# Token-major gates for the 'b' heads, multiplied on GpSimd and turned by DMA transposes in a split-f16 encoder block

## The chip, the cores and the metric

The kernel runs on one core of a Trainium2 chip, as one launch. The metric is the device time of a launch in microseconds (us), lower is better; it is given as the median of several runs. The core has five engines with queues of their own: PE (TensorE, matrix multiplications out of a stationary operand that PEld loads), DVE (VectorE), ACT (ScalarE), POOL (GpSimd) and SP (SyncE, which issues nearly all DMAs here). Each engine runs its instructions in the order in which they stand in the program and waits at each one for what it needs.

## The reference, cut to what matters

One encoder layer on 1024 tokens of width 1024: a combined projection `x @ w_in`, two groups of eight attention heads of 64 columns each, gates, an output projection, and a normalisation.

```python
h = x @ w_in
q_a, k_a, v_a, z_a, q_b, k_b, v_b, z_b = split(h)
y_a = neighborhood_attention(q_a, k_a, v_a, rel_pos_bias)      # 8 heads, window of 8 x 16 tokens of a 16 x 64 grid
y_b = windowed_gqa_with_sink(rotary(q_b), rotary(k_b), v_b, sink_logits)   # 8 query heads, 2 key heads, |i - j| <= 128
mixed = concatenate([y_a * silu(z_a), y_b * silu(z_b)])
y = mixed @ w_out
x = layer_norm(DEEPNORM_ALPHA * x + y, ln_gain, ln_bias)
```

The change touches `y_b * silu(z_b)` and the way in which that product reaches `mixed @ w_out`.

## The kernel before, in words

**Arithmetic.** Large products are made of f16 parts: a value is split into a high and a low f16 part, and a product takes three passes (high by high, high by low, low by high). `x` and `w_in` are split so; so are the softmax weights, and the gated outputs `zt[e]` for `W_out` (`mh[e]`, `ml[e]`). There are eight gated tiles of 128 columns (two heads) by 1024 tokens, f32: `zt[0..3]` for the 'a' heads, `zt[4..7]` for the 'b' heads.

**Projection.** The 21 groups of 128 columns of `w_in` (without the values, which are projected apart) are computed in the order `ORDER`. `project` (L358, matmul at L379) makes a group channel-major: a 128x128 weight tile is the stationary operand, 512 tokens of `x` move past it, and the result stands with the 128 columns on the partitions. A group is two halves of 512 tokens, each 8 steps of the contraction by three passes, so 48 matmuls of 512 columns. The weights of a group come as two pieces of 512 of the contraction rows (`w_split`, L191): ACT makes the high part (L199), POOL scales and subtracts for the low part (L204, L205). In `project`, the second piece is needed only at the thirteenth matmul of a half. `evac` (L318) reads the result out of PSUM: for a gate, `Silu` on ACT for the first three groups of `ORDER`, and otherwise `Tanh` on ACT (L341) with a product on DVE (L342). A 'b' query group (`qb0` to `qb3`) is rotated by `rope` (L305): a copy on ACT, a shuffle on DVE (L312), then two products and a sum on POOL (L313 to L315), after which ACT casts the high part of each head (L259) and POOL subtracts for the low part (L265).

**Prologue and steps.** The values and the first `NPRO = 6` groups of `ORDER` run before the attention (the last rows of the values end at 59 us). Then 128 units of attention follow, units 0 to 63 for 'b' and 64 to 127 for 'a'; a unit is one head with 128 queries. The 15 other groups are filler: `pump_to` puts their matmuls between those of the units by the marks `FILL_AT`. The loop that sets the order is the step loop at L1180: step `i` emits the scores of unit `i` (`stage_qk`: L816, L817 on PE, then the masked sum and minimum on DVE, L826), the exponential of unit `i` on ACT (L842), and for unit `i - 1` the split of its weights into f16 parts (`stage_tr`: high part on ACT L852, low part on DVE L853) and a DMA transpose of both parts, issued by SP (L856). Every fourth step a quad `q` of four units gets its product with the values (`stage_pv`, L881 on PE) some `LP = 6` steps later, and is normalised on DVE (`stage_on`, L887 and L890) into the tile `on`, f32, tokens on the partitions. When both heads of a pair are there, `stage_ot` (L893) turns the tile `on` by four f32 transposes on PE (L901) into PSUM, and DVE multiplies by the gate and writes `zt[e]` (L904 for 'b', one instruction over 128x512; L910 for 'a', two over 128x256).

The scores of unit `i + 4` use the PSUM bank of unit `i`; they wait for the split of that unit (L852, L853), which reads that bank.

**Side work.** What isn't written into the step by hand stands in four queues (`act`, `dve`, `pool`, `sp`): `enq` adds an operation with those it depends on and a priority, and `pop` takes, at its place in a step, a few operations whose dependencies were emitted in earlier steps. `need` emits an operation at once. The weights of `W_out` are loaded, scaled and split there too. `m_queue(e)` (L1009), called at the steps `M_AT = [105, 112, 118, 120]` for `e = 4..7`, splits the gated 'b' tiles: a cast on ACT (L1013) and a subtraction on POOL (L1014) for each half. The 'a' tiles are split at the end (`final`, L1048, by L938 and L939).

**Output.** `out_mms` (L1021, matmul at L1031) multiplies `W_out`: stationary are 128 tokens of `mh[e]` or `ml[e]`, and 512 columns of `W_out` move (128 or 256 in the last pieces). Most of it runs behind the last unit. The normalisation and the stores end the program.

**Buffers that matter here.** `zslot` gives slots for gate tiles; the gain and the bias of the normalisation took such slots at the end, and the gain's load waited for `m_ops[4]` (L1207). The tag `bs` (`BR = 5` buffers) holds the 'a' heads' bias tables, loaded a few steps ahead by `stage_load`.

Of the kernel before, what the change touches and what calls it, by code (L numbers as in the profile page):

```python
# [15 lines left out]
S = 1024  # L16
# [20 lines left out]
ZTAG = {"z3": "zv", "zb3": "zc", "z2": "zs", "zb1": "zd", "zb2": "ze"}  # L37
KO = (2, 3, 4, 5, 6, 7, 0, 1)
X1_AT = ((0,), (1,), (2,), (3, 4), (5,), (6, 7), (), ())
Z3_END = 119  # L40
# [21 lines left out]
def hybrid_block(ctx, tc, xT, x, wt, wv, wo, bias, sink, gain, lbias, cos, sin, bmask, out):  # L62
# [33 lines left out]
    def zslot(name, tag="z"):  # L96
        return zp.tile([128, S], F32, tag=tag, name=name, bufs=3 if tag == "z" else 1)
# [247 lines left out]
        return [o2]  # L345

    def z_col(e):
        i = 0 if e in (4, 0, 5) else 1 if e == 1 else 2
        return zc[:, i:i + 1]

    groups = []
# [1 line left out]
    def new_group():  # L353
        if len(groups) >= 2:
            need(*groups[-2])
        return bank("pj")

    def project(name):  # L358
        n = ORDER.index(name)
        w_split(2 * n + 2)  # L360
        for half in range(2):
            ps = new_group()
            for k in range(KT):
                if k % 4 == 0:
                    need(w_ops[2 * n + k // 4])
                h, l = parts[2 * n + k // 4]
                if n + 2 < NPRO and half == 0 and k == 4:
                    w_scan(2 * n + 4)
                if n + 2 < NPRO and half == 1 and k == 0:
                    w_scan(2 * n + 5)  # L370
                if half == 0 and k == 4:
                    w_split(2 * n + 3)
                if n + 2 < NPRO and half == 1 and k == 6:
                    w_scale(n + 2)
                for i, (a, b) in enumerate(((h, x16h), (h, x16l), (l, x16h))):
                    mv = b[half, k]
                    if name[0] == "q" and name[1] != "b":
                        mv = mv.rearrange("p (r b c) -> p b r c", b=4, r=8)
                    nc.tensor.matmul(ps, a[:, k % 4, :], mv,  # L379
                                     start=(k == 0 and i == 0), stop=(k == KT - 1 and i == 2))  # L380
# [482 lines left out]
    def stage_pv(q):  # L863
        ps = st[q, "o"] = bank("t")
        for m in range(4):
# [14 lines left out]
            for i, (a, b_) in enumerate(mms):  # L880
                nc.tensor.matmul(ps[:, HD * m:HD * m + HD], a, b_, start=(i == 0), stop=(i == len(mms) - 1))  # L881

    def stage_on(q):
# [6 lines left out]
        nc.vector.tensor_mul(on[g, p, h][:, :, j, :], ps[:, :4 * HD].rearrange("p (m e) -> p m e", e=HD),  # L890
                             ri.unsqueeze(2).to_broadcast([128, 4, HD]))

    def stage_ot(q):  # L893
        g, p, j, h = quad(q)
        if j == 0:
            return
        need(*stk_ops.get(f"zb{p}" if g == "b" else f"z{p}", ()))
        ps = bank("t")
        o = on.pop((g, p, h))
        for i in range(4):  # L900
            nc.tensor.transpose(ps[:, 128 * i:128 * i + 128], o[:, i].rearrange("p h e -> p (h e)"), identf)  # L901
        if g == "b":
            z = zt[4 + p][:, 512 * h:512 * h + 512]
            nc.vector.scalar_tensor_tensor(z, ps, z_col(4 + p), z, op0=ALU.mult, op1=ALU.mult)  # L904
        else:
            for i in range(2):
                b = 2 * h + i
                z = zt[p].rearrange("p (r c) -> p r c", c=GW)[:, :, 16 * b:16 * b + 16]
                src = ps[:, 256 * i:256 * i + 256].rearrange("p (r c) -> p r c", c=16)
                nc.vector.scalar_tensor_tensor(z, src, z_col(p), z, op0=ALU.mult, op1=ALU.mult)  # L910

    for b in range(4):
        at(WIN_AT[b], window, b)
# [15 lines left out]

    def m_alloc(e):  # L930
        if e >= 4:
            t = big_tile(f"m{e}", (128, 2, S), F16)
        else:
            t = tiles["fp"].tile([128, 2, S], F16, tag="m", name=f"m{e}", bufs=4)
        mh[e], ml[e] = t[:, 0, :], t[:, 1, :]

    def m_split(e, sl, hi, lo):
        hi(mh[e][:, sl], zt[e][:, sl])  # L938
        lo(ml[e][:, sl], zt[e][:, sl], mh[e][:, sl])  # L939
# [69 lines left out]
    def m_queue(e):  # L1009
        m_alloc(e)  # L1010
        m_ops[e] = []
        for h in (slice(0, 512), slice(512, S)):
            o = enq("act", lambda h=h: nc.scalar.copy(mh[e][:, h], zt[e][:, h]))  # L1013
            m_ops[e].append(enq("pool", lambda h=h: nc.gpsimd.tensor_sub(  # L1014
                ml[e][:, h], zt[e][:, h], mh[e][:, h]), o))

    LT, LP = LTT, LPP
    LO = LP + 4
# [1 line left out]
    NU = len(units)  # L1020
    def out_mms(t, a, ps, es, c=(0, 512)):  # L1021
        o, w = c
        ts, cs = slice(128 * t, 128 * t + 128), slice(o, o + w)
        ps = ps[:, o:o + w]
        for e in es:
            n = WO_SEQ.index((e, a))
            if n in wo_ops:
                need(wo_ops[n], *m_ops.get(e, ()))
            woh, wol = wo_parts[n]
            for i, (lh, rh) in enumerate(((mh[e], woh), (mh[e], wol), (ml[e], woh))):  # L1030
                nc.tensor.matmul(ps, lh[:, ts], rh[:, cs],  # L1031
                                 start=(e == EO[0] and i == 0), stop=(e == EO[-1] and i == 2))
                yield

# [13 lines left out]
    def final():  # L1048
# [5 lines left out]
        for e in EO[4:]:  # L1054
            m_alloc(e)
        for e in EO[4:]:
            m_split(e, slice(0, 512), nc.scalar.copy, nc.vector.tensor_sub)
            for n in (WO_SEQ.index((e, 0)), WO_SEQ.index((e, 1))):
                wo_split(n)
        for e in EO[4:]:  # L1060
            m_split(e, slice(512, S), nc.scalar.copy, nc.vector.tensor_sub)
# [112 lines left out]
    gain_tile = []  # L1174

    def gain_load():
        gain_tile.append(zslot("gb"))
        nc.sync.dma_start(gain_tile[0], gain.partition_broadcast(128))

    clock["step"] = 0  # L1180
    for i in range(-LD, NU + LO):
# [59 lines left out]
        pop("dve", ND if i < M_AT[1] else 2, same=True)  # L1241
        if i < NU:
            stage_exp(units[i])
        pop("act", NA if i < M_AT[0] and len(queues["act"]) < 5 else 2)
        pop("pool", NP)
        pump_to(i + 1)
    pump(10 ** 6)
# [77 lines left out]
```

## Time and profile before

| What | Value |
|---|---|
| Median of 3 runs | 445.71 us (445.67 to 446.71) |
| The profiled execution's own time | 446.49 us |
| Its span in the profile | 444.7 us |
| Mean granted TensorE clock | 0.995 |
| DMA traffic | 81.39 MB, 133841 packets |

A program on one core has one row of each kind. The page gives times in us from the start of the span, and single durations in ns. In the groups of instructions, the last columns are the group's busy time, the mean duration of one, and idle time of the engine in front of them with what ended it. Matmuls overlap: the next one starts before the one before has ended, so their cost is read from how far apart they start, or from the chain of waits, where a run of them appears as one piece. The profiled execution took 1.8 us more than its span, which lies around it.

### The profile page before, as it was taken

The numbers are of one execution on the slowest core, as the hardware profiler recorded it, in microseconds if no ns is written. First come the engines' busy times: TensorE is split into PE (matmuls) and PEld (weight loads), VectorE is DVE, ScalarE is ACT, GpSimd is POOL, SyncE is SP. The second block draws the span as 40 slices with busy tenths as digits, with TensorE's granted clock in tenths as the row PEclk, the third lists the DMA queues.
The fourth block names the chain that finished last, engine by engine and source line by source line (L and its number), as shares of the span: only waits on it lengthen the run. The fifth ranks groups of instructions, "written<-read, shape, count | busy, mean of one in ns | idle before, by whom it ended". The sixth has DMA issues, their size and how long they took to land.

```text
span 444.7 us, 9505 instructions
## 1 busy us (share of the span) xinstructions
PE 437.5 (98%) x3289; PEld 255.5 (57%) x3289; DVE 344.2 (77%) x849; ACT 308.3 (69%) x700; POOL 221.6 (50%) x235
## 2 busy tenths in 40 slices
PE   9999999999999999999999999999999999999994
PEld 8997754444445565655565655656555654444453
DVE  5978967438986898887988888888878837589944
ACT  5759789766499988887868887888778946302401
POOL 0110074646839558866506767765574405205740
PEclk9999999999999999999999999999999999999997
DMA  8921469984659999587978899998999998103612
GB/s 272 390 91 60 145 235 339 336 292 169 213 127 214 206 190 181 98 162 143 164 127 175 169 182 180 213 170 213 192 204 253 167 172 347 55 0 102 232 69 72
DMA packets 133841, 81.39 MB, mean 183 GB/s; under 512 B 101280, under 2 KB 113440, under 8 KB 133536
## 3 DMA queue, kind: packets, MB, share of 16 engines
q1 hardware_dynamic: 133648, 80.64, 75.4%
q8 instruction: 26, 0.43, 0.4%
q14 instruction: 23, 0.19, 0.2%
q10 hardware_dynamic: 144, 0.13, 0.1%
HBM read 50.34 MB, written 9.96 MB: 136 GB/s over the span
## 4 chain that ended last, share of the span: by engine, by line
PE 91%; DMA 3%; POOL 3%; DVE 1%; issue 1%; ACT 1%; SPq 0%; POOLq 0%; DVEq 0%; ACTq 0%
PE ps_pj L379 44%; PE ps_s L1031 9%; PE ps_s L486 6%; PE ps_t L881 6%; PE ps_pj L1031 5%; PE ps_t L1031 5%; PE ps_s L816 4%; PE ps_s L817 4%; PE ps_pj L486 3%; PE ps_t L486 3%; DMA bias<-in_bias 3%; PE ps_t L901 1%; POOL wl L205 1%; PE ps_t L412 1%; POOL ks L295 1%
## 5 line engine op out<-in xcount | busy, mean ns | idle before, releaser
L379 PE MATMUL ps_pj<-xf,wh 128*128 128x512 f16 x672 | 202.1, 379 | 0.1
L379 PE MATMUL ps_pj<-xf,wl 128*128 128x512 f16 x336 | 127.3, 379 | 0.0
L379 PEld LDWEIGHTS <-wh 128*128 128x128 f16 x672 | 63.7, 98 | 60.4 <-DVE ks L263 0.5
L842 ACT ACTIVATE ps_s<-sn,nm 128x385 f32<-128x385 f32 (+3 forms) x128 | 70.1, 548 | 25.1 <-DVE nm L826 24.6
L853 DVE SCALAR_TENSOR_TENSOR split<-ps_s,split 128x384 f16<-128x384 f32 (+2 forms) x128 | 65.7, 513 | 27.5 <-ACT split L852 25.9
L1031 PEld LDWEIGHTS <-m 128*128 128x128 f16 x432 | 40.0, 98 | 41.1 <-DVE m L939 0.2
L852 ACT ACTIVATE split<-ps_s 128x384 f16<-128x384 f32 (+2 forms) x128 | 57.8, 452 | 2.5 <-DMA tr<-split 0.2
L204 POOL TENSOR_SCALAR wr<-wr,wsc 128x512 f32<-128x512 f32 x26 | 20.6, 791 | 68.1 <-ACT wh L199 61.6
L379 PEld LDWEIGHTS <-wl 128*128 128x128 f16 x336 | 32.9, 98 | 37.4
L826 DVE CUSTOM_DVE_ANT_0 sn<-ps_s,bm,nsk 128x384 f32<-128x384 f32 (+1 forms) x64 | 40.7, 636 | 2.0 <-PE ps_s L817 1.7
L1031 PE MATMUL ps_s<-wo,m 128*128 128x512 f16 (+1 forms) x192 | 40.8, 366 | 0.0
L816 PE MATMUL ps_s<-ks,qs 128*128 128x384 f16 (+4 forms) x128 | 39.2, 306 | 0.3 <-DVE qs L263 0.3
L817 PE MATMUL ps_s<-ks,qs 128*128 128x384 f16 (+4 forms) x128 | 39.2, 306 | 0.0
L826 DVE CUSTOM_DVE_ANT_0 sn<-ps_s,bias,sg 128x264 f32<-128x264 f32 (+1 forms) x64 | 35.0, 547 | 4.5 <-issue 1.5
L881 PEld LDWEIGHTS <-tr 128*128 128x128 f16 (+1 forms) x1104 | 36.6, 98 | 2.2
L205 POOL TENSOR_TENSOR wl<-wr,wh 128x512 f16<-128x512 f32 x26 | 32.7, 1257 | 2.2
L788 POOL TENSOR_SCALAR bias<-bias,rsg 128x552 f32<-128x552 f32 (+1 forms) x24 | 19.1, 797 | 23.8 <-DMA bias<-in_bias 22.6
L295 POOL COPY ks<-ks 64x512 f16<-64x512 f16 x40 | 26.0, 661 | 7.1 <-DVE ks L263 2.8
L1086 ACT ACTIVATE sd<-mv,eps 128x1 f32<-128x1 f32 x8 | 2.4, 295 | 36.5 <-DVE mv L1084 35.2
L1031 PE MATMUL ps_pj<-wo,m 128*128 128x512 f16 (+1 forms) x144 | 26.2, 326 | 0.0
L1130 POOL TENSOR_TENSOR xr<-xr,gb 128x512 f32<-128x512 f32 x7 | 9.8, 1396 | 32.4 <-ACT xr L1127 32.4
L842 ACT ACTIVATION_READ_ACCUMULATOR ps_s<-sn,nm 128x1 f32 x128 | 24.4, 190 | 0.0
(188 smaller groups left out, 813.8 us busy)
## 6 DMA issues: line engine op xcount, KB each, us to landing
ws<-in_wt SPq DMA_DIRECT2D x15, 512.0 KB, 5.9
wr<-in_wt SPq DMA_DIRECT2D x26, 256.0 KB, 3.6
wor<-in_wo SPq DMA_DIRECT2D x22, 256.0 KB, 3.5
bias<-in_bias SPq DMA_DIRECT2D x16, 276.0 KB, 3.3
xr<-in_x SPq DMA_DIRECT2D x8, 512.0 KB, 9.6
out<-xr SPq DMA_DIRECT2D x15, 256.0 KB, 2.1
bias<-in_bias SPq DMA_DIRECT2D x8, 368.0 KB, 3.8
wvraw<-in_wv SPq DMA_DIRECT2D x9, 320.0 KB, 5.8
```

The costliest lines, as they stand in the source:

```text
L205: nc.gpsimd.tensor_sub(l, raw, h)
L295: nc.gpsimd.tensor_copy(t[o, sl], t[a, sl])
L379: nc.tensor.matmul(ps, a[:, k % 4, :], mv, start=(k == 0 and i == 0), stop=(k == KT - 1 and i == 2))
L486: nc.tensor.matmul(ps[:, :320], lh[:, ts], rh[:, cs], start=(k == ko[0] and i == 0), stop=(k == ko[-1] and i == 2))
L816: nc.tensor.matmul(ps[:, :m], q, sl[0], start=True, stop=False)
L817: nc.tensor.matmul(ps[:, :m], q, sl[1], start=False, stop=True)
L826: nc.vector.tensor_tensor_reduce(sn[:, :m], ps[:, :m], bias_t, sg[:, c:c + 1], init, op0=ALU.add, op1=ALU.min, accum_out=nm)
L842: nc.scalar.activation(pt[:, :m], sn[:, :m], AF.Exp, bias=nm, scale=-1.0, accum_out=sm[:, k:k + 1])
L852: nc.scalar.activation(hl[:, :m, 0, :c], src, AF.Copy, scale=PSCALE)
L853: nc.vector.scalar_tensor_tensor(hl[:, :m, 1, :c], src, PSCALE, hl[:, :m, 0, :c], op0=ALU.mult, op1=ALU.subtract)
L881: nc.tensor.matmul(ps[:, HD * m:HD * m + HD], a, b_, start=(i == 0), stop=(i == len(mms) - 1))
L1031: nc.tensor.matmul(ps, lh[:, ts], rh[:, cs], start=(e == EO[0] and i == 0), stop=(e == EO[-1] and i == 2))
```

## The change

1. **Projection of the 'b' gates.** `zb0` to `zb3` are made by a new `project_rows`, token-major: a tile of 128 tokens of `x` is the stationary operand and the 128 weight columns move, so a group is 2 x 96 matmuls of 128 columns, with four blocks of tokens one behind the other. Each block goes through all of the contraction, so both weight pieces are needed at the start.
2. **Order.** The groups of the prologue are now zb0, zb1, zb2, kb, qb0, zb3; `z0` and `z1` take the places of `zb2` and `zb3` in the filler.
3. **Gate of 'b'.** `stage_on` multiplies on DVE by the scale of the gate and by one over the sum in one instruction, and a POOL product (`tensor_mul`, 128x256, 16 of them, priority 0.6) multiplies the gate tile by it, tokens on the partitions. `stage_ot` does nothing for 'b': 32 f32 transposes on PE and the 8 DVE products of L904 are gone.
4. **f16 parts of 'b'.** `m_queue` runs at `M_AT = [26, 42, 57, 80]`. For each half, ACT casts the high part and POOL subtracts the low part, both into a tile `hr`, token-major; then SP issues a DMA transpose of 128x1024 f16 that writes the two parts channel-major into `zt[e]` itself. The `hr` tiles take buffers of the tag `bs` (for `e = 7` the gate slot `zv`). `mh`, `ml` are views with a stride.
5. **Ends.** The steps from which two queued operations may be taken stay as they were (`POP2_AT`). The gain and the bias of the normalisation stand in large tiles of their own, and the gain's load waits for nothing.

```diff
-ORDER = ["zb0", "z0", "zb1", "kb", "qb0", "z1", "qb1", "zb2", "qb2", "k0", "qb3", "zb3", "q0", "k1", "q1",
+ORDER = ["zb0", "zb1", "zb2", "kb", "qb0", "zb3", "qb1", "z0", "qb2", "k0", "qb3", "z1", "q0", "k1", "q1",
...
-M_AT = [105, 112, 118, 120]
+M_AT = [26, 42, 57, 80]
+POP2_AT = (105, 112)
...
+    def project_rows(name):
+        n = ORDER.index(name)
+        w_split(2 * n + 2)
+        for half in range(2):
+            ps = new_group()
+            need(w_ops[2 * n], w_ops[2 * n + 1])
+            for c in range(96):
+                t, k, i = c // 24, c // 3 % 8, c % 3
...
+                ts = slice(128 * t, 128 * t + 128)
+                h, l = parts[2 * n + k // 4]
+                a, b = ((x16h, h), (x16l, h), (x16h, l))[i]
+                nc.tensor.matmul(ps[:, ts], a[half, k][:, ts], b[:, k % 4, :], start=(c % 24 == 0), stop=(c % 24 == 23))
+                if c % 4 == 3 and c < 95:
+                    yield
+            groups.append(evac(name, half, ps))
+            yield
...
-        nc.vector.tensor_mul(on[g, p, h][:, :, j, :], ps[:, :4 * HD].rearrange("p (m e) -> p m e", e=HD),
-                             ri.unsqueeze(2).to_broadcast([128, 4, HD]))
+        o, src = on[g, p, h][:, :, j, :], ps[:, :4 * HD].rearrange("p (m e) -> p m e", e=HD)
+        rb = ri.unsqueeze(2).to_broadcast([128, 4, HD])
+        if g == "a":
+            nc.vector.tensor_mul(o, src, rb)
+            return
+        nc.vector.scalar_tensor_tensor(o, src, z_col(4 + p), rb, op0=ALU.mult, op1=ALU.mult)
+        z = zt[4 + p].rearrange("p (t j e) -> p t j e", j=2, e=HD)[:, 4 * h:4 * h + 4, j, :]
+        gate_ops.setdefault(4 + p, []).append(enq("pool", lambda: nc.gpsimd.tensor_mul(z, z, o), prio=0.6))
 
     def stage_ot(q):
         g, p, j, h = quad(q)
-        if j == 0:
+        if j == 0 or g == "b":
             return
...
-        if g == "b":
-            z = zt[4 + p][:, 512 * h:512 * h + 512]
-            nc.vector.scalar_tensor_tensor(z, ps, z_col(4 + p), z, op0=ALU.mult, op1=ALU.mult)
...
     def m_alloc(e):
         if e >= 4:
-            t = big_tile(f"m{e}", (128, 2, S), F16)
+            t = zt[e].bitcast(F16).rearrange("p (t i c) -> p t i c", i=2, c=128)
+            mh[e], ml[e] = t[:, :, 0, :], t[:, :, 1, :]
...
-        for h in (slice(0, 512), slice(512, S)):
-            o = enq("act", lambda h=h: nc.scalar.copy(mh[e][:, h], zt[e][:, h]))
-            m_ops[e].append(enq("pool", lambda h=h: nc.gpsimd.tensor_sub(
-                ml[e][:, h], zt[e][:, h], mh[e][:, h]), o))
+        if e == 7:
+            whole = zslot("hr7", "zv").bitcast(F16).rearrange("p (t i f) -> p t i f", i=2, f=128)
+        for h in range(2):
+            hr = whole[:, 4 * h:4 * h + 4] if e == 7 else ap.tile([128, 4, 2, 128], F16, tag="bs", name=f"hr{e}{h}", bufs=BR)
+            z = zt[e][:, 512 * h:512 * h + 512].rearrange("p (t f) -> p t f", f=128)
+            out16 = zt[e].bitcast(F16).rearrange("p (n c) -> p n c", c=128)[:, 8 * h:8 * h + 8, :]
+            o = enq("act", lambda hr=hr, z=z: nc.scalar.copy(hr[:, :, 0, :], z), *gate_ops[e])
+            o = enq("pool", lambda hr=hr, z=z: nc.gpsimd.tensor_sub(hr[:, :, 1, :], z, hr[:, :, 0, :]), o)
+            m_ops[e].append(enq("sp", lambda hr=hr, out16=out16: nc.sync.dma_start(
+                out16, hr.rearrange("p t i f -> p (t i f)"), transpose=True), o))
...
-                nc.tensor.matmul(ps, lh[:, ts], rh[:, cs],
+                nc.tensor.matmul(ps, lh[:, t, :], rh[:, cs],
...
-        gb, bb = gain_tile[0], zslot("bb")
+        gb, bb = gain_tile[0], big_tile("bb", (128, D), F32)
...
-            enq("sp", gain_load, *m_ops[4])
+            enq("sp", gain_load)
```

More of the change, by code (lines that the diff above doesn't have):

```diff
@@ L347, in z_col @@
     def z_col(e):
[L348 removed]
+        i = 0 if e in (4, 5, 6) else 1 if e == 7 else 2
         return zc[:, i:i + 1]
@@ L356, in new_group @@
         return bank("pj")
+    def project_rows(name):
[6 more added lines that the diff above has]
+                t, k, i = c // 24, c // 3 % 8, c % 3
+                if n + 2 < NPRO and (half, c) == (0, 48):
+                    w_scan(2 * n + 4)
+                if n + 2 < NPRO and (half, c) == (1, 0):
+                    w_scan(2 * n + 5)
+                if (half, c) == (0, 48):
+                    w_split(2 * n + 3)
+                if n + 2 < NPRO and (half, c) == (1, 72):
+                    w_scale(n + 2)
+                ts = slice(128 * t, 128 * t + 128)
[6 more added lines that the diff above has]
+            yield
     def project(name):
+        if name[:2] == "zb":
+            yield from project_rows(name)
+            return
         n = ORDER.index(name)
@@ L901, in stage_ot @@
             nc.tensor.transpose(ps[:, 128 * i:128 * i + 128], o[:, i].rearrange("p h e -> p (h e)"), identf)
-        if g == "b":
-            z = zt[4 + p][:, 512 * h:512 * h + 512]
[L904 to L910, printed above, removed]
+        for i in range(2):
+            b = 2 * h + i
+            z = zt[p].rearrange("p (r c) -> p r c", c=GW)[:, :, 16 * b:16 * b + 16]
+            src = ps[:, 256 * i:256 * i + 256].rearrange("p (r c) -> p r c", c=16)
+            nc.vector.scalar_tensor_tensor(z, src, z_col(p), z, op0=ALU.mult, op1=ALU.mult)
     for b in range(4):
@@ L1022, in out_mms @@
         o, w = c
-        ts, cs = slice(128 * t, 128 * t + 128), slice(o, o + w)
+        cs = slice(o, o + w)
         ps = ps[:, o:o + w]
@@ L1056, in final @@
         for e in EO[4:]:
-            m_split(e, slice(0, 512), nc.scalar.copy, nc.vector.tensor_sub)
+            m_split(e, slice(0, 4), nc.scalar.copy, nc.vector.tensor_sub)
             for n in (WO_SEQ.index((e, 0)), WO_SEQ.index((e, 1))):
@@ L1240, in hybrid_block @@
             stage_on(q)
-        pop("dve", ND if i < M_AT[1] else 2, same=True)
+        pop("dve", ND if i < POP2_AT[1] else 2, same=True)
         if i < NU:
             stage_exp(units[i])
-        pop("act", NA if i < M_AT[0] and len(queues["act"]) < 5 else 2)
+        pop("act", NA if i < POP2_AT[0] and len(queues["act"]) < 5 else 2)
         pop("pool", NP)
```

17 lines of the change are left out of this document (10 added, 7 removed).

## The prediction

> **What bounds the kernel now.** I read the page first: busy shares, the slices with the granted clock, and the chain of work that ended last.
>
> ```profile
> span 444.7 us, 9505 instructions
> ...
> PE 437.5 (98%) x3289; PEld 255.5 (57%) x3289; DVE 344.2 (77%) x849; ACT 308.3 (69%) x700; POOL 221.6 (50%) x235
> ...
> PEclk9999999999999999999999999999999999999997
> ...
> PE 91%; DMA 3%; POOL 3%; DVE 1%; issue 1%; ACT 1%; SPq 0%; POOLq 0%; DVEq 0%; ACTq 0%
> PE ps_pj L379 44%; PE ps_s L1031 9%; PE ps_s L486 6%; PE ps_t L881 6%; PE ps_pj L1031 5%; PE ps_t L1031 5%; PE ps_s L816 4%; PE ps_s L817 4%; PE ps_pj L486 3%; PE ps_t L486 3%; DMA bias<-in_bias 3%; PE ps_t L901 1%; POOL wl L205 1%; PE ps_t L412 1%; POOL ks L295 1%
> ```
>
> PE is the bound, at full clock but for the last slice. The other engines matter only where they make PE wait. The table by stages (start and end, length, then busy us of PE, PEld, DVE, ACT, POOL with instruction counts, clock, DMA share, GB/s) shows how near they are in the steps of the 'b' heads, 121 to 237 us:
>
> ```profile
> 121.00:160.00 39.00, 39.00 (x312) 21.36 (x311) 31.04 (x88) 35.60 (x93) 24.22 (x23) 1.00 0.90 173
> 160.00:200.00 40.00, 40.00 (x350) 22.92 (x348) 35.24 (x102) 32.67 (x83) 29.92 (x32) 1.00 0.83 162
> 200.00:237.00 37.00, 37.00 (x333) 21.15 (x332) 31.70 (x89) 28.06 (x71) 17.12 (x18) 1.00 0.82 150
> 237.00:265.00 28.00, 27.90 (x264) 16.19 (x262) 23.86 (x66) 22.37 (x60) 19.17 (x25) 1.00 0.86 165
> ```
>
> PE never rests, but ACT is at 91% in the first of them, DVE at 88% in the second, POOL at 75% there. So work taken from PE pays in full only while the chain that feeds it keeps up: scores, minimum (DVE), exponential (ACT), split (ACT, DVE).
>
> **The change on PE.** Three pieces of the chain of waits (start, length, engine, tile, line, count) give the prices; the chain charges overlapping matmuls by their spacing.
>
> ```profile
> 68.72 10.38 PE ps_pj L379 x48
> ...
> 165.00 0.44 PE ps_t L901 x4
> ...
> 434.25 2.69 PE ps_pj L1031 x48
> ```
>
> Removed: 32 f32 transposes at 0.44 / 4 = 0.11 us: 3.5 us. Exchanged: four groups of 48 matmuls of 512 columns, 10.38 us each, for four of 192 matmuls of 128 columns. The last piece is just that shape, f16, a fresh stationary tile for each: 2.69 / 48 = 0.056 us, so 10.76 a group and 0.38 more; for four, 1.5 us more. Net gain on PE: 3.5 - 1.5 = 2.0 us, and by span plus what lies around it, 446.49 - 2.0 = 444.5.
>
> The Trainium skill's page "TensorE: Matmul & The Clock Gate", section "Back-to-back issue gap", speaks against this: it gives a stream of weight loads and 128-column matmuls about 81 ns each, and 56 ns only for an isolated one. By it the four groups would take 62 us in place of 41.5, an estimate of some 19 us more than by the row. The row of 48 above is such a stream, at 56.
>
> **The start.** Each token block of `zb0` needs both weight pieces at once; before, the second piece was wanted at the thirteenth matmul. The timeline (start, length, engine, line):
>
> ```profile
> 59.27 1.16 POOL L205 TENSOR_TENSOR wl<-wr,wh 128x512 f16<-128x512 f32 x1
> ...
> 59.37 0.59 PE L379 MATMUL ps_pj<-xf,wh 128*128 128x512 f16 x2
> ```
>
> The low part of the second piece ends at 60.43. Its first use in the new order is about the fifteenth 128-column matmul, 59.37 + 14 x 0.056 = 60.15. PE waits 0.3 to 0.5 us, I take 0.4. Later groups' pieces are made a group ahead.
>
> **Work moved on the other engines.** Rows from the groups by line:
>
> ```profile
> L890 DVE TENSOR_TENSOR on<-ps_t,ri x32: 423/424/426, 141.1 to 365.8; 128x256 f32<-128x256 f32 x32
> L904 DVE SCALAR_TENSOR_TENSOR z<-ps_t,zc,z x8: 744/746/751, 159.4 to 257.9; 128x512 f32<-128x512 f32 x8
> L910 DVE SCALAR_TENSOR_TENSOR z<-ps_t,zc,z x16: 472/476/485, 280.8 to 369.9; 128x256 f32<-128x256 f32 x16
> L1014 POOL TENSOR_TENSOR m<-z,m x8: 1157/1160/1166, 329.4 to 348.4; 128x512 f16<-128x512 f32 x8
> L1013 ACT CAST m<-z x8: 602/610/618, 320.7 to 347.1; 128x512 f16<-128x512 f32 x8
> L1099 POOL TENSOR_TENSOR xr<-xr,gb x1: 728/728/728, 433.1 to 433.1; 128x256 f32<-128x256 f32 x1
> ```
>
> DVE loses 8 x 0.746 = 6.0 us and pays at most 16 x (0.476 - 0.424) = 0.8, if the two-product form costs what L910 does. POOL gets 16 products of 128x256, by L1099 0.73 each, 11.6 us. The eight casts (4.9 us) and eight subtractions (9.3 us) move from steps 105 to 125 to steps 26 to 85. POOL goes over the 'b' steps from about 71 us busy in 116 to about 90, nearly 80%; ACT from 96 to about 100. In the 'a' steps both are relieved, but PE did not stall on the casts there, so nothing is gained. DMA transposes are new on SP:
>
> ```profile
> L856 SPq DMA_TRANSPOSE tr<-split x128: 1188/1212/2615, 126.1 to 361.3; - x128
> ...
> DMA to landing us min/median/max: 2.5/3.4/6.2
> ```
>
> Eight of about 1.2 us on SP stand ahead of a unit's own transpose, one or two at a time, and behind them the units' transposes and the loads of SP. The last transpose of a tight quad, issued by SP, and the first use by L881 (the loads on PEld):
>
> ```profile
> 139.14 2.50 SPq L856 DMA_TRANSPOSE tr<-split  x2
> ...
> 142.77 1.16 PEld L881 LDWEIGHTS <-tr 128*128 128x128 f16 x33
> ```
>
> 3.6 us of room where landing takes 3.4. So one issue ahead of such a transpose costs PE up to 1.2 us, and up to 2.6, the longest issue in the row, if it also waits; ahead of the first three transposes of a quad, which are due as late as the fourth, it costs nothing. I take nothing and keep the rest for the range.
>
> **Where POOL's new product sits.** The order of POOL's instructions after the change is qs, product, qs, L313, L314, weights L204 and L205, L315. Before, in this place:
>
> ```profile
> 139.33 2.38 POOL L265 TENSOR_TENSOR qs<-rp_raw,qs 64x512 f16<-64x512 f32 x2
> ...
> 141.07 0.42 DVE L890 TENSOR_TENSOR on<-ps_t,ri 128x256 f32<-128x256 f32 x1
> ...
> 141.79 1.27 POOL L313 TENSOR_TENSOR rp_raw<-rp_raw,cos 128x512 f32<-128x512 f32 x1
> ...
> 146.16 1.28 POOL L315 TENSOR_TENSOR rp_raw<-rp_raw,rp_sw 128x512 f32<-128x512 f32 x1
> ...
> 147.48 0.62 ACT L259 CAST qs<-rp_raw 64x512 f16<-64x512 f32 x1 [0.75 <-POOL rp_raw L315]
> ...
> 148.00 0.48 ACT L852 ACTIVATE split<-ps_s 128x384 f16<-128x384 f32 x1
> ...
> 148.52 0.56 DVE L853 SCALAR_TENSOR_TENSOR split<-ps_s,split 128x384 f16<-128x384 f32 x1 [1.06 <-ACT split L852]
> ...
> 149.41 0.33 PE L816 MATMUL ps_s<-ks,qs 128*128 128x384 f16 x1
> ```
>
> The first qs ends at 140.5; the product waits for DVE until 141.5, runs to 142.2, and the second qs to 143.4: L313 starts 1.6 to 1.7 us late, with no gap before L315 to take it up. ACT already waited 0.75 for L315 and stands in order: cast, split L852, exponential and DVE's L853 all come 1.7 later. L853 ended at 149.08 and freed the bank that L816 wants at 149.41; it would end at 150.75, and PE waits 1.3 us. This is the one stall that I can place. Elsewhere the same chain has more room (rows below), except around the change from 'b' to 'a' heads, where the splits end just ahead of PE's need:
>
> ```profile
> 240.52 0.56 DVE L853 SCALAR_TENSOR_TENSOR split<-ps_s,split 128x384 f16<-128x384 f32 x1 [0.78 <-ACT split L852]
> ...
> 241.29 0.31 PE L816 MATMUL ps_s<-ks,qs 128*128 128x352 f16 x1
> ```
>
> 0.2 us of room (L853 ends at 241.08). The casts of `e = 6` (0.61 us each, two) and two extra issues on SP fall at steps 59 to 62 just ahead of it, and only one L904 goes from DVE there. I put 0 to 1.2 us there and take 0.5, nearer the lower end, as ACT idles some 20% in that stage.
>
> **The sum.** 446.5 - 2.0 + 0.4 + 1.3 + 0.5 = 446.7 by the profiled execution, 0.2 over its own time. That execution lay 446.49 - 445.71 = 0.8 over the median, so 445.9 against the median: no change. Under 0.3%, 1.3 us, this measurement can't tell from none. Its own range, with both stalls at their ends (0 to 1.7 and 0 to 1.2): 444.3 to 447.0.
>
> **The rivals.** (a) All of PE's gain is kept: 445.7 - 2.0, and with the start's 0.4, 443.7 to 444.1; I take 443.9. For it: DVE loses 5 us of work in the 'b' steps, which speeds the chain that feeds PE, and an unhindered chain may take up the 1.7 us. Against it: ACT's measured 0.75 us wait for POOL at the very place. (b) Slower: POOL becomes the engine on which ACT stands. Six half rotations run in the steps:
>
> ```profile
> L313 POOL TENSOR_TENSOR rp_raw<-rp_raw,cos x6: 1265/1269/1278, 133.0 to 204.6; 128x512 f32<-128x512 f32 x6
> ```
>
> Each can be held up by a product or a pair of subtractions, 0.73 to 2.3 us, and ACT, in order, holds exponential and split behind its cast. If three more such holds reach PE with 1.0 to 1.4 us each, the sum is 445.9 + 3 x 1.2 = 449.5; from one and a bit on (447.0) it counts as slower. For it: POOL near 80%, and SP's extra issues in just these steps. Against it: an ordinary unit's split ends 1.7 us ahead of PE's need, and POOL has gaps that take up a delay:
>
> ```profile
> 145.59 0.56 DVE L853 SCALAR_TENSOR_TENSOR split<-ps_s,split 128x384 f16<-128x384 f32 x1
> ...
> 147.89 0.27 PE L816 MATMUL ps_s<-ks,qs 128*128 128x256 f16 x1
> ...
> 163.00 1.27 POOL L313 TENSOR_TENSOR rp_raw<-rp_raw,cos 128x512 f32<-128x512 f32 x1 [3.07 <-DVE rp_sw L312]
> ```
>
> One such hold gives 447.1, three 449.5; I price it at two, 448.3.
>
> (c) The stream of 128-column matmuls is bound by its weight loads:
>
> ```profile
> L1031 PEld LDWEIGHTS <-m 128*128 128x128 f16 x432 | 40.0, 98 | 41.1 <-DVE m L939 0.2
> ```
>
> A load takes 98 ns by itself. If 768 in a row did not overlap as the 48 did, they would be spaced up to 98 ns, 768 x (0.098 - 0.056) = 32 us more, and 16 at half of that: about 462. Against it: the 48, of the same shape and type. The page of the Trainium skill cited above stands for it.
>
> (d) The change doesn't do what it says: PE had no work in place of the transposes, and the steps go at the pace of ACT and DVE, so only the dearer projection is left, 445.7 + 1.5 = 447.2.
>
> **How the numbers follow.** Forecast 0.33, (a) 0.31, (b) 0.28, (c) 0.04, (d) 0.04. The time is the likeliest's, 445.9. Range: from 443.5, just under (a), to 449.6, which holds (b) up to three holds; left out are (c), the tail of (b) and a little below (a), 0.15 to 0.2. Faster by over 0.3% (under 444.4) is (a) with a little of the forecast, 0.32; slower (over 447.0) is (b), (c), most of (d) and a little of the forecast, 0.37; within, 0.31.
>
> **What would show it.** The new matmul line's piece of the chain: 10.7 to 10.8 us per group and no f32 transposes in the 'b' steps. At the start an idle PE of 0.4 released by POOL's low part. About unit 17, PE idle of 1 us or more ahead of the scores, released by DVE's split, with ACT waiting for POOL's L315 longer than 0.75; if this wait is there and PE does not idle, the forecast's step fails and (a) holds. Idle PE ahead of L881 released by a DMA would show SP's part. A piece per group over 11 us would speak for (c); PE idle of over 4 us in the 'b' steps for (b).

## The result and the profile after

The changed kernel takes 458.48 us (median of 6 runs, 457.85 to 460.71) beside 445.91 for the kernel before on the same chip: a ratio of 1.0286 (95% interval 1.0264 to 1.0308), 12.6 us slower. The profiled execution took 458.51 us with a span of 456.7, 12.0 over the span before.

The page's first lines and its chain of waits, by engine:

```profile
span 456.7 us, 10609 instructions
...
PE 438.3 (96%) x3833; PEld 275.7 (60%) x3833; DVE 342.6 (75%) x841; ACT 308.4 (68%) x700; POOL 232.9 (51%) x251
...
PE 66%; DVE 9%; POOL 8%; ACT 6%; issue 5%; DMA 5%; POOLq 0%; DVEq 0%; SPq 0%; ACTq 0%
```

PE's share of the chain fell from 91% to 66%: the end is now held by other engines for a third of the span. What PE waits for is told by the view of waits (engine, tile, line, releaser: us in total, times, longest):

```profile
PE ps_t L1006 <- DVE wom L997: 4.8, 1, 4.8
PE ps_s L845 <- DVE split L882: 4.3, 4, 1.7
PE ps_t L910 <- DMA tr<-split: 2.3, 6, 0.7
PE ps_t L1152 <- ACT dr L1150: 1.8, 1, 1.8
PE ps_t L441 <- DVE warm L128: 1.0, 1, 1.0
```

The last two stand in the kernel before too; the first three, 11.4 us, are new. The first comes from a place that the prediction doesn't name. `wo_scale` sets the scale of `W_out` from the sums of absolute values of the rows of all its 16 pieces (the expectations below call these sums maxima), and its small matmul L1006 stopped until DVE had made the last piece's sums (L997). SP, PE and DVE there, in the timeline (start, length, engine, line, operation, output and inputs, shape, count, idle time before it and what ended it):

```profile
214.92 1.23 SPq L1055 DMA_TRANSPOSE z<-hr  x1
...
219.80 1.26 SPq L1055 DMA_TRANSPOSE z<-hr  x1
...
224.36 0.57 SPq L986 DMA_DIRECT2D wor<-in_wo  x1
...
227.09 0.38 PE L408 MATMUL ps_pj<-xf,wl 128*128 128x512 f16 x1
...
230.77 0.69 DVE L264 SCALAR_TENSOR_TENSOR qs<-ps_pj,qs 64x512 f16<-64x512 f32 x1
...
231.50 0.69 DVE L997 TENSOR_REDUCE wom<-wor 128x1 f32<-128x512 f32 x1
232.24 0.18 PE L1006 MATMUL ps_t<-wom,ones 128*128 128x16 bf16 x1 [4.77 <-DVE wom L997]
...
232.50 0.84 PE L408 MATMUL ps_pj<-xf,wh 128*128 128x512 f16 x2
```

The piece's load was issued by SP at 224.36. Two of the new transposes stood ahead of it in the queue from which a step takes one DMA. The same load before:

```profile
211.78 0.53 SPq L951 DMA_DIRECT2D wor<-in_wo  x1
```

Counted in units whose scores PE had begun, the load went out at unit 49 before and at unit 53 here; without the transposes (run 3 below) it was 49 again. So the sums slid in DVE's order until they stood right in front of the scale. PE had begun three units whose splits DVE had not ended; here it stops until DVE has worked off its row, 4.8 us. Behind the stop six matmuls of 512 columns took 2.38 us, where they take 1.29 elsewhere:

```profile
232.66 2.38 PE ps_pj L408 x6
...
200.00:237.00 37.00, 30.23 (x232) 15.61 (x229) 27.08 (x81) 26.55 (x67) 24.41 (x24) 0.95 0.84 154
```

The first row is from the chain, the second from the table by stages: the granted clock was 0.95 in this stage, 1.00 before. That costs another 1.7 us, by the matmuls' spacing.

The other new waits, in order of time:

```profile
150.65 0.62 ACT L260 CAST qs<-rp_raw 64x512 f16<-64x512 f32 x1 [2.62 <-POOL rp_raw L316]
152.29 0.32 PE L845 MATMUL ps_s<-ks,qs 128*128 128x384 f16 x1 [1.73 <-DVE split L882]
...
191.96 0.35 PE L910 MATMUL ps_t<-vb,tr 128*128 128x64 f16 x6 [0.30 <-DMA tr<-split]
199.69 0.43 PE L910 MATMUL ps_t<-vb,tr 128*128 128x64 f16 x9 [0.42 <-DMA tr<-split]
...
212.58 0.69 ACT L342 ACTIVATE z<-ps_pj,invt 128x512 f32<-128x512 f32 x1 [2.06 <-POOL rp_raw L314]
215.11 0.32 PE L845 MATMUL ps_s<-ks,qs 128*128 128x384 f16 x1 [1.60 <-DVE split L882]
```

The first pair is the stop at unit 17 that was forecast. The two rows of L910 are quads whose product waits until the DMA transpose of their weights has landed, that is, has written its data. The last pair is a stop that the prediction doesn't have: ACT's tanh of `z1` stands in the memory of the cosine table (`ZTAG`, "zc") and waits until POOL's last rotation has read it. The same wait, then of the tanh of `zb3`, stood in the kernel before and cost PE nothing there:

```profile
205.87 0.69 ACT L341 ACTIVATE z<-ps_pj,invt 128x512 f32<-128x512 f32 x1 [1.75 <-POOL rp_raw L313]
```

The token-major groups cost what was forecast:

```profile
68.59 10.74 PE ps_pj L378 x192
```

Laid against each PE instruction's usual spacing, the new stops and the slow stretch add 15.6 us (0.3 at the start, 1.9 at unit 17, 1.1 at 186 to 190, 1.8 and 0.6 at 213 and 222, 4.9 at L1006 and 1.7 of low clock behind it, 3.3 for transposes of quads over the whole span), and the work of PE is 2.0 less. Two parts differ from one execution to the next and not by the change: the first 20 us took 0.8 less (in run 1, a changed kernel, as long as before), and the stretch behind the last matmul with `W_out` took 7.2 us where the profiled execution of before had 8.0 (in run 2, nearly the kernel before, 7.2). The sum, 15.6 - 2.0 - 0.8 - 0.8 = 12.0, is the difference of the spans.

### The profile page after: what moved, and what is told of

It reads as the page before. It is cut to its first block, busy times and chain, and to the rows that moved or that the text cites. A ratio compares the mean times of both kernels' runs of the same rounds, so it can differ in the third digit from the quotient of the medians.

```text
span 456.7 us, 10609 instructions
## 1 busy us (share of the span) xinstructions
PE 438.3 (96%) x3833; PEld 275.7 (60%) x3833; DVE 342.6 (75%) x841; ACT 308.4 (68%) x700; POOL 232.9 (51%) x251
## 4 chain that ended last, share of the span: by engine, by line
PE 66%; DVE 9%; POOL 8%; ACT 6%; issue 5%; DMA 5%; POOLq 0%; DVEq 0%; SPq 0%; ACTq 0%
PE ps_pj L408 20%; PE ps_s L1072 9%; PE ps_pj L378 7%; PE ps_s L515 6%; PE ps_pj L1072 5%; PE ps_t L910 5%; PE ps_t L1072 5%; PE ps_pj L515 3%; PE ps_s L845 2%; PE ps_s L846 2%; POOL wl L206 2%; DMA bias<-in_bias 2%; DMA tr<-split 2%; ACT split L881 2%; ACT ps_s L871 2%
## 5 line engine op out<-in xcount | busy, mean ns | idle before, releaser
L408 PE MATMUL ps_pj<-xf,wh 128*128 128x512 f16 x544 | 165.1, 381 | 0.0
L408 PE MATMUL ps_pj<-xf,wl 128*128 128x512 f16 x272 | 103.6, 381 | 0.0
L408 PEld LDWEIGHTS <-wh 128*128 128x128 f16 x544 | 51.7, 98 | 45.9 <-issue 0.8
L408 PEld LDWEIGHTS <-wl 128*128 128x128 f16 x272 | 26.8, 98 | 30.3 <-issue 0.6
L378 PEld LDWEIGHTS <-xf 128*128 128x128 f16 x768 | 43.2, 98 | 0.6 <-issue 0.3
L378 PE MATMUL ps_pj<-wh,xf 128*128 128x128 f16 x512 | 43.4, 219 | 0.0
L378 PE MATMUL ps_pj<-wl,xf 128*128 128x128 f16 x256 | 43.2, 219 | 0.2 <-POOL wl L206 0.2
L910 PEld LDWEIGHTS <-tr 128*128 128x128 f16 (+1 forms) x1104 | 37.0, 98 | 6.1 <-DMA tr<-split 3.0
L1072 PEld LDWEIGHTS <-m 128*128 128x128 f16 x216 | 20.2, 98 | 21.4 <-DVE m L974 0.2
L1072 PEld LDWEIGHTS <-z 128*128 128x128 f16 x216 | 20.0, 98 | 19.7
```

The lines of the kernel that those rows point to most:

```text
L378: nc.tensor.matmul(ps[:, ts], a[half, k][:, ts], b[:, k % 4, :], start=(c % 24 == 0), stop=(c % 24 == 23))
L408: nc.tensor.matmul(ps, a[:, k % 4, :], mv, start=(k == 0 and i == 0), stop=(k == KT - 1 and i == 2))
L1072: nc.tensor.matmul(ps, lh[:, t, :], rh[:, cs], start=(e == EO[0] and i == 0), stop=(e == EO[-1] and i == 2))
```

## The experiments

Every ratio is against runs of the kernel before on the same chip, whose medians lay between 445.86 and 446.78.

**1. The scale of W_out later.**

```diff
-WO_SCALE = 55
+WO_SCALE = 59
```

> Kernel after, with the scale of W_out computed at step 59 in place of 55, so that the last maximum of W_out's rows (its load now stands behind two of the new transposes on SP) is long done when PE wants it. Theory 1: the 4.8 us wait of PE on that maximum and the slow clock behind it (1.5 us) are a cost of their own, so 458.5 - 6.3 = 452.2, between 451.5 and 453. Rival, theory 2: POOL and SP are overloaded in the 'b' steps and the wait only lets them catch up; other waits grow in its place and the time stays above 456.

Measured 454.96, ratio 1.0196 (1.0171 to 1.0221): by the ratios 4.0 us of the 12.6, between the two theories. The wait at L1006 is gone; at 236 to 250 us PE now loses 2.5 us to late splits, transposes and key parts, where it lost nothing behind the stop.

**2. The same wait put into the kernel before**, by one number in `WO_LD`: the ninth load at step 51.

```diff
-WO_LD = [16, 22, 19, 25, 36, 39, 42, 45, 48, ...
+WO_LD = [16, 22, 19, 25, 36, 39, 42, 45, 51, ...
```

> Kernel before, with the load for the last maximum of W_out's rows queued at step 51 in place of 48, so that the maximum stands on DVE right ahead of the scale, as in the kernel after; nothing else changes. Theory 1: PE waits 4 to 5 us there as in the kernel after and runs at a lower clock behind it, 445.9 + 5 to 6.5 = 451 to 452.5. Theory 2: the wait needs the overload of the 'b' steps, so before stays at 446 to 447.

Measured 451.24, ratio 1.0104 (1.0086 to 1.0122), the lower end of theory 1. The waits of PE and the stage:

```profile
PE ps_t L971 <- DVE wom L962: 3.9, 1, 3.9
...
200.00:237.00 37.00, 33.10 (x271) 18.01 (x270) 28.29 (x81) 24.73 (x61) 14.43 (x14) 0.91 0.66 133
```

So the wait needs nothing of the change but the late load.

**3. No parts work.** The casts, subtractions and DMA transposes that make the f16 parts of 'b' are left out; `m_queue` only writes zeros, at the old steps.

```diff
-M_AT = [26, 42, 57, 80]
+M_AT = [105, 112, 118, 120]
...
+        m_ops[e] = [enq("pool", lambda: nc.gpsimd.memset(zt[e], 0.0))]
+        return
```

> Kernel after, leaving out the f16 parts of the four gated 'b' tiles (the eight casts, subtractions and DMA transposes); zeros written by POOL at steps 105 to 120 stand in their place, so W_out multiplies zeros for 'b'. Theory 1: the wait on W_out's last maximum is gone (the load is no longer behind transposes on SP), and so are the waits at 185 to 199 and 213 to 222 us; left are the start (0.3) and the wait near unit 17 (1.9): about 446.5 to 448. Theory 2 (POOL's products are what overloads the 'b' steps): above 452.

Measured 452.09, ratio 1.0123 (1.0106 to 1.014). The number is at the edge of theory 2, but not by its mechanism alone: parts work costs some 7 us in all, the wait at L1006 among it. The stops at 185 to 199 went, but the one at 212 did not (1.9 us, and half speed behind it): it isn't made by the casts, subtractions or transposes of the parts.

**4. Products on DVE**: `nc.vector.tensor_mul(z, z, o)` in place of the queued POOL product.

> Kernel after, with the 16 gate products on DVE right behind the normalisation in place of POOL (in step order, some 0.5 us each). Theory 1: the wait near unit 17 (1.9 us, POOL's rope late by the product) goes, and part of the one at 213 us; the wait on W_out's last maximum stays: 455 to 457. Theory 2: POOL's load is the cause of most of the loss, 448 to 452. Third: DVE is nearer the path than POOL, and it gets slower than 458.5.

Measured 461.53, ratio 1.0334 (1.0299 to 1.037): the third case. PE waits 7.1 us for splits in eight places. The wait at L1006, which theory 1 kept, is not in this profile (the load went out at unit 51), so the products on DVE cost more than the 3 us between the two medians. Relieving POOL by loading DVE is a loss here; the feeding chain runs over DVE.

**5. Three POOL operations a step** (`NP = 3`, on top of run 1).

> Kernel after with the scale of W_out at step 59 (455.0 by itself), and three queued operations of POOL a step in place of two. Theory 1 (the gate product takes one of a step's two places, so the query's subtractions and the rotations stand a step later on POOL and ACT waits behind them): POOL's last rotation comes earlier and the 2.4 us wait of PE at 212 us shrinks, 452.5 to 454; the wait near unit 17 (1.5) stays, as the product stands ahead of the rotation still. Theory 2 (POOL's load itself): no change, 454.5 to 455.5.

Measured 457.16, ratio 1.0261 (1.0236 to 1.0285), worse than both theories. The stop at 212 shrank to 0.5, but PE waited 6.7 us for transposes of quads in place of 2.1. The first two new transposes go out 2.7 us apart with one of the units' between them, in run 1 4.4 us apart with two between; that this is what makes the quads late is argued, not shown.

**6. Products last**: priority 1 in place of 0.6, on top of run 1.

> As with the scale at step 59, and the gate products at priority 1 in place of 0.6, so that rotations and query splits that wait already go first on POOL. Theory 1: both waits of PE that POOL's order makes go, unit 17 (1.5) and 212 us (2.4): 455.0 - 3.9 = 451.1, 450.5 to 452.5. Theory 2 (POOL's load): what is gained there comes back in later waits, above 453.5.

Measured 452.81, ratio 1.0149 (1.0125 to 1.0173), between the two. At unit 17 nothing is left; the stop at 211 us shrank from 2.4 to 1.4. The last load ahead of the scale goes out here while PE is at unit 51 and its sums are made while PE is at unit 53, ahead of step 55, so products last alone might have taken away the wait at L1006; that wasn't run.

**7. z1 behind q0**, on top of run 1.

```diff
-"qb3", "z1", "q0", "k1", "q1",
+"qb3", "q0", "z1", "k1", "q1",
```

> As with the scale at step 59, and the gate group z1 projected after q0 in place of before it. z1's tile stands in the memory of the cosine table, so ACT's tanh of z1 waits until POOL's last rotation has read the table. Theory 1: that wait of ACT (2.4 us) is what stops PE at 212 us; with z1 later it is gone and so is PE's stop: 455.0 - 2.4 = 452.6, 452 to 453.5. Theory 2: ACT's wait isn't what PE waits for there, 454.5 to 455.5.

Measured 454.27, ratio 1.0179 (1.0146 to 1.0211): inconclusive by the time. In the profile the stop at 212 shrank from 2.4 to 1.0, but a late transpose of a quad cost 2.1 at 234.46, with half speed behind it.

**8 and 9. The products alone, in the kernel before**, first at priority 0.6 and then at 1.

```diff
+        if g == "b":
+            o = on[g, p, h][:, :, j, :]
+            if q == 0:
+                st["pm"] = ap.tile([128, 4, HD], F32, tag="bs", name="pm", bufs=BR)
+            w = st["pm"]
+            enq("pool", lambda: nc.gpsimd.tensor_mul(w, o, o), prio=0.6)
```

> Kernel before, with 16 products of 128x256 on POOL added behind the normalisation of the 'b' heads (a square of its result into memory that nothing reads, priority 0.6); nothing else changes. Theory 1: these products alone make the two waits of PE, near unit 17 (1.3 to 1.9 us) and at the tanh in the cosine table's memory (about 2): 446.0 + 3 to 4 = 449 to 450. Theory 2 (the waits need the other parts of the change, since PE's lead is smaller there): under 447.

> Kernel before with the same 16 added POOL products as in the run with priority 0.6 (450.3), at priority 1. Theory 1: the place of the product ahead of the rotation and the query splits is the cost, not its 0.73 us of POOL: unit 17's stop goes and the time is 446 to 447.5. Theory 2: POOL's load is the cost: 449 to 450.5.

Measured 450.27, ratio 1.01 (1.0081 to 1.012), and 447.67, ratio 1.0018 (1.0005 to 1.0032). The cast of ACT near unit 17, first at priority 0.6 and then at 1, from the timelines:

```profile
149.20 0.62 ACT L259 CAST qs<-rp_raw 64x512 f16<-64x512 f32 x1 [2.51 <-POOL rp_raw L315]
```

```profile
147.65 0.62 ACT L259 CAST qs<-rp_raw 64x512 f16<-64x512 f32 x1 [1.32 <-POOL rp_raw L315]
```

The same 11.6 us of POOL (16 products at 0.73) cost 4.4 us in one place of its order and 0.9 in another: theory 1 of run 9, most of the cost is the place and not the load. Of the 4.4 us the wait at unit 17 is 1.3; the rest are smaller waits, the largest 0.7 for a quad's transpose at 321.6. One half of run 8's expectation fell: no stop at 212 appears in it; that one needs the rest of the change.

**10. No parts work, products last** (run 3 with priority 1; run 3 is the expectation's "second run").

> Without the f16 parts work of 'b' (zeros by POOL in its place, as in the second run, 452.1) and with the gate products at priority 1. Theory 1 (of what is left, POOL's order makes the stops): unit 17 (1.3) and 212 us (2.1 and 1.5 of lower clock behind it) go, 452.1 - 4.9 = 447.2, 446.5 to 448.5. Theory 2 (some other engine paces the steps once PE has less to do): above 450.5.

Measured 450.18, ratio 1.0075 (1.006 to 1.009), between the two: unit 17 is clean, the stop at 210 is 1.8. Three fifths of the loss that run 3 left are still there.

**11. No transposes** (run 6 with the SP operation left out and zeros written later).

> As with the scale at step 59 and the products at priority 1 (452.8), leaving out the eight DMA transposes of the parts: casts and subtractions stay, and zeros written by POOL at steps 105 to 120 stand in zt[4..7]. Theory 1: SP's eight issues cost PE only its waits for landings in the 'b' steps (0.7 at 189 us, 0.5 at 221 us), 451 to 452. Theory 2: SP, nearly full, is what paces the steps, and the casts and subtractions cost little: 447.5 to 450.

Measured 449.81, ratio 1.0063 (1.0048 to 1.0078), theory 2: against run 6 the eight transposes cost 0.0086 x 446 = 3.8 us, some 1.3 either way by the two intervals. The waits of L910 for landings, 2.8 us in run 6 at five places between 189 and 360, are gone.

**12. Work spread** (run 6 with z1 behind q0 and `M_AT = [32, 48, 70, 84]`).

> As with the scale at step 59 and the products at priority 1 (452.8), with z1 projected after q0 and the parts queued at steps 32, 48, 70 and 84, so that no cast or subtraction falls into a half rotation or the change from 'b' to 'a'. Theory 1: the stop at 211 us (1.4) and those of 0.3 to 0.6 at 236 to 245 us go, 450 to 451.5, still over before. Theory 2: the work shifts the stops to where it stands now, 452.3 to 454.

Measured 453.76, ratio 1.0155 (1.0137 to 1.0174), theory 2: the splits' stops shrank to 0.6 and less, and PE waited 5.3 us for transposes instead.

**13. No parts work, products last, z1 behind q0.**

> Without the f16 parts work of 'b', products at priority 1 (450.2 beside a before of 446.8, ratio 1.0075), and z1 projected after q0. Theory 1: the 1.8 us stop at 210 us is ACT's tanh waiting for the cosine table, and goes: ratio 1.0025 to 1.0045. Theory 2 (POOL's load delays the query splits whoever waits): 1.006 or more.

Measured 448.34, ratio 1.0049 (1.003 to 1.0068), just above theory 1, with both theories' ranges in the interval: against run 10 z1's tanh was worth 1.2 us, hardly beyond the two intervals. In the profile the stop at 210 shrank from 1.8 to 0.3.

**14. Neither parts nor products** (run 3 with the products left out too).

```diff
-        gate_ops.setdefault(4 + p, []).append(enq("pool", lambda: nc.gpsimd.tensor_mul(z, z, o), prio=1))
+        gate_ops.setdefault(4 + p, [])
```

> The kernel after leaving out both the f16 parts work of 'b' (zeros by POOL at steps 105 to 120) and the 16 gate products: left are the token-major projection, the new order of groups, the missing transposes and the new normalisation. Theory 1: PE keeps its 2.0 us less 0.3 at the start, ratio 0.995 to 0.998, since POOL is as free as before. Theory 2 (the steps are paced by ACT, DVE or SP once PE has less to do): ratio 0.999 to 1.003.

Measured 448.96, ratio 1.0073 (1.0052 to 1.0095): outside both. With nothing added to POOL and SP in the 'b' steps, the kernel is slower than before. The timeline of DVE, ACT and PE:

```profile
171.11 0.69 DVE L997 TENSOR_REDUCE wom<-wor 128x1 f32<-128x512 f32 x1 [2.89 <-DMA wor<-in_wo]
...
172.43 0.59 ACT L871 ACTIVATE ps_s<-sn,nm 128x385 f32<-128x385 f32 x1 [2.08 <-DVE nm L855]
...
209.58 0.69 ACT L342 ACTIVATE z<-ps_pj,invt 128x512 f32<-128x512 f32 x1 [1.75 <-POOL rp_raw L314]
...
212.10 0.32 PE L845 MATMUL ps_s<-ks,qs 128*128 128x384 f16 x1 [1.33 <-DVE split L882]
```

DVE stands in front of another piece's sums of `W_out` and waits 2.9 us for the load. The splits' ends, counted from the first scores of unit 0, are 0.7 us earlier than before at unit 24 and 1.5 later at unit 25, and stay 1.1 to 1.7 late until unit 51 (the two traces against each other); PE, 0.4 to 1.3 us earlier than before in these units because it has no transposes, runs into them: 1.3 us at 212, and 2.3 in smaller stops at 227 to 274. The load landed late; the range of landings at 163 to 172 us, before and in run 14:

```profile
DMA to landing us min/median/max: 2.9/3.2/3.4
```

```profile
DMA to landing us min/median/max: 3.3/4.3/5.2
```

Run 2, whose program is the kernel before up to this place, had the load late too (4.1 us to landing), and DVE waited for it:

```profile
168.15 0.69 DVE L962 TENSOR_REDUCE wom<-wor 128x1 f32<-128x512 f32 x1 [1.29 <-DMA wor<-in_wo]
```

PE did not stop behind it in run 2. The landing varies without the change, and PE's room took it up.

**15. The full kernel with the scale later, products last, z1 behind q0.**

> The full kernel after with the scale at step 59, the products at priority 1 (ratio 1.015) and z1 projected after q0. Theory 1: the 1.4 us stop at 211 us goes and the repairs add up, ratio 1.010 to 1.013. Theory 2: it stays at 1.014 to 1.018, as with z1 later and the parts shifted (1.0155).

Measured 450.64, ratio 1.0105 (1.009 to 1.012), theory 1: the repairs add up. What is left, from the waits of PE:

```profile
PE ps_t L910 <- DMA tr<-split: 5.5, 8, 1.9
```

**16 and 17. The sums of `W_out`'s rows two steps later behind their loads**, in run 14 (with z1 behind q0 and the scale at 59) and in run 15.

```diff
+                load_ops["wo", n].lag = 4
```

> Without the parts work and the products (zeros by POOL in place of the parts; ratio 1.0073), with z1 after q0, the scale at step 59, and DVE's maxima of W_out's rows taken two steps later behind their loads, so that DVE never waits for one. Theory 1: PE's saving of 2.0 us less the start's 0.3 comes out: ratio 0.995 to 0.998. Theory 2 (with PE's transposes gone ACT and DVE pace the 'b' steps in any case): 0.999 to 1.003.

> The full kernel with all repairs: the scale at step 59, products at priority 1, z1 after q0 (ratio 1.0105), and the maxima of W_out's rows two steps later behind their loads. Theory 1: the wait of DVE (1.0 us) goes, 1.006 to 1.009, and what is left is PE waiting for late transposes of quads. Theory 2: no change, as these transposes pace it: 1.0095 to 1.012.

Measured 446.13, ratio 0.9987 (0.9971 to 1.0002), and 450.36, ratio 1.0085 (1.0053 to 1.0116). In the profiled execution of run 16 (443.95 us, the fastest of its twelve) PE doesn't rest in the steps of 'b':

```profile
121.00:160.00 39.00, 39.00 (x339) 22.21 (x336) 30.91 (x86) 34.65 (x91) 24.13 (x24) 1.00 0.83 170
160.00:200.00 40.00, 40.00 (x343) 22.13 (x342) 35.55 (x102) 33.78 (x86) 30.95 (x33) 1.00 0.92 167
200.00:237.00 37.00, 37.00 (x331) 20.68 (x329) 32.12 (x91) 29.07 (x74) 18.59 (x19) 1.00 0.87 156
```

There the span is 442.1, 2.6 under before, but not all of that is the change: 0.5 lies ahead of the first projection and 0.8 behind the last matmul with `W_out`. Between them PE saves 1.3 us, where 2.0 less 0.4 at the start was forecast. Over the twelve runs the median is 0.5 us under before, and the interval allows -1.3 to +0.1: how much of it shows in a usual run isn't settled, and the ratio lies between the two theories. In the full kernel the last repair can't be told from none: run 17's ratio fits theory 1, its interval takes in theory 2, and its profile shows 5.8 us of waits for transposes of quads, which both named. No changed kernel with the whole computation came below 448.1 in any run.

## Why the prediction was wrong

Forecast was 445.9 with a range up to 449.6. Point by point:

- **PE's work** was right: 10.74 us a group against 10.76, 0.32 at the start against 0.4. The profile of run 16 has 1.3 us of PE's saving, with the start's wait taken off.
- **Unit 17** was right in place and cause (POOL's product ahead of the rotation, then ACT, then the split): 1.7 us against 1.3, because POOL's rotation had slipped by 2.2 us against the steps and not by 1.7. Runs 6, 8 and 9 confirm the cause: the stop goes with the product's place in POOL's order.
- **The failed step is the one on SP.** The prediction says that behind the new transposes stand "the units' transposes and the loads of SP", prices only the landing of a quad's last transpose, and takes nothing for it. Two things were wrong. The loads were named and nobody asked who waits for them: one is `W_out`'s last piece, DVE's sums of it stand in PE's way at `wo_scale`, and this cost 4.0 us by run 1, 4.8 in the kernel before by run 2. And the transposes themselves, whose landings were taken at nothing, were worth 3.8 us by run 11, with the scale later and the products last. The prediction names 1.2 and 2.6 us for a single issue and keeps them "for the range", but no bound of its range is made of them.
- **"Elsewhere the same chain has more room"** was read from the profile of before, with PE at its old pace. Every 0.44 us that PE saves is taken from that room. By unit 44 PE is 1.3 us nearer to the splits (run 14), and waits of DVE or ACT that cost nothing before (the tanh in the cosine table's memory, a late load) become stops of PE. Run 2 has such a late load in the kernel before, without a stop. That is theory 2 of run 14 in the form that fits: not a lack of speed of ACT and DVE, since run 16's profiled execution goes through these steps without stops, but single waits in their order. Run 16 makes three changes to run 14 at once; what each is worth there wasn't run.
- **Rival (b)** had the right direction and the right first link, POOL's order, but it stopped at 449.5; POOL's part is about 2 us by runs 1 and 6. It names SP's extra issues, but not as a mechanism of its own with a price. Rival (a), all of PE's gain kept, comes near to what run 16's profile shows, but without the work that the change needs. Rival (d), steps at the pace of ACT and DVE, doesn't fit that profile, in which PE doesn't rest. Rival (c) is refuted: 192 matmuls of 128 columns stand in one piece of 10.74 us, at 56 ns. By the Trainium skill, page "TensorE: Matmul & The Clock Gate", section "Back-to-back issue gap", it would have been some 81 ns; the trace disagrees.
- **The tight spot** at the change to 'a' cost nothing in the kernel after, and 2.5 us in run 1 without the stop at 232, which had, it seems, let the others catch up. Costs of this kind need not add.

Taken in the order of the repairs (ratios times 446): scale 4.0, products last 2.1, z1 behind q0 2.0, loads later 0.9 (not beyond its interval), and the parts and products themselves, run 17 against run 16, 4.4. In another order the shares would differ, as the note on run 6 says of the scale. It isn't shown what makes the landing at 171 us late, and a repair of SP's issues wasn't tried.

## What to carry to other kernels

When an engine gets new work, list for each of its queues not only what is delayed but who waits for the delayed thing, to the end: a load behind a new DMA, the reduction that reads it, the matmul that needs the reduction. Room read from a profile belongs to the pace of that profile; work taken from the bounding engine shortens the room everywhere behind it, so ask which wait of the feeders is longest, not only which is tight now. A queued operation's price is its place in the order: the same POOL products cost 4.4 us where they stood ahead of the rotations and 0.9 where they stood behind them.

## What the runs showed of the hardware that was not expected

A stop of PE was followed by half speed in some cases: matmuls of 512 columns 0.43 us apart, in place of 0.22, after 4.8 us (kernel after), 3.9 us (run 2), 2.1 us (run 7) and 1.9 us (run 3), but not after 2.0 us in run 11, nor after 2.3 us in run 1 at the same place as in run 3.

```profile
214.23 0.32 PE L845 MATMUL ps_s<-ks,qs 128*128 128x384 f16 x1 [1.94 <-DVE split L882]
...
215.51 1.04 PE L408 MATMUL ps_pj<-xf,wh 128*128 128x512 f16 x2
```

```profile
214.60 0.32 PE L845 MATMUL ps_s<-ks,qs 128*128 128x384 f16 x1 [2.27 <-DVE split L882]
...
215.89 0.59 PE L408 MATMUL ps_pj<-xf,wh 128*128 128x512 f16 x2
```

The first is run 3, the second run 1: two matmuls take 1.04 us and 0.59. The granted clock from 200 to 237 us was 0.95 in run 3 and 1.00 in run 1. The Trainium skill, page "TensorE: Matmul & The Clock Gate", section "What's actually happening", has the clock fall after an idle window of about 3.4 us that runs free of the kernel; the halving agrees, while the stop of 1.9 us is shorter than that.
